# Loading the first four groups of an RMSNorm-GELU kernel as two transfers with 64 KB pieces, and gamma as one

## The chip, the cores and the metric

The kernel runs on one core of one Trainium2 chip. The metric is the device time of one execution in microseconds; lower is better. All executions quoted here are fast (granted clock 1.00). The profiled span of an execution is about 2 us shorter than the time by the clock. Each kernel has one profiled execution: that of the kernel before took 317.25 us. DVE is the vector engine, ACT the scalar engine, PE the matrix engine; SP only issues transfers here.

## The reference

```python
# x: (8, 1024, 2048) float32, gamma: (2048,) float32, eps = 1e-5
rms = np.sqrt(np.mean(x ** 2, axis=-1, keepdims=True) + eps)
out = gamma * x / rms
return 0.5 * out * (1 + np.tanh(np.sqrt(2 / np.pi) * (out + 0.044715 * out ** 3)))
```

8192 rows of 8 KB are read once and written once: 67.1 MB in, 67.1 MB out, and little arithmetic on each element.

## The kernel before

The rows are cut into 16 groups of 512. A group is one SBUF tile of 128 partitions with four rows (32 KB) each. Six such tiles ("slots") are reused in turn: load g+6 may start when store g has landed. Loads are issued from SP, stores from ACT.

```python
ROWS, SLOTS, GW, CHUNK, NARROW = 4, 6, 64, 1024, 128
...
x3 = x.rearrange("b s d -> (b s) d").rearrange("(g p r) d -> g p r d", p=P, r=R)
slot = [sbuf.tile([P, R, D], FP32, name=f"slot{i}") for i in range(SLOTS)]
flat_pieces = {0: [(0, NARROW), (NARROW, R * D)]}   # store 0 only: a 512 B piece per partition, then the rest

def load(g):
    nc.sync.dma_start(out=slot[g % SLOTS], in_=x3[g])
...
def gelu_store(g):
    # four GELU activations on ACT, one per row, then:
    for a, b in flat_pieces.get(g, [(0, R * D)]):
        nc.scalar.dma_start(out=dst[:, a:b], in_=flat[:, a:b])
...
for k in range(0, D, CHUNK):                        # gamma in two transfers of 4 KB
    nc.scalar.dma_start(out=gamma_row[...], in_=gamma[k : k + CHUNK]...)
for g in range(SLOTS):
    load(g)
# PE spreads gamma to 128 partitions in PSUM (L142)
for g in range(G + 1):
    if g < G:
        # squares of group g: two or three rows on ACT (L72), one or two on DVE (L82)
        # inverse root (L90 to L102; the power on GpSimd, L95), scale by gamma on DVE (L109)
    if g:
        gelu_store(g - 1)                           # L120, L127
        if g - 1 + SLOTS < G:
            load(g - 1 + SLOTS)                     # L68
```

The store of group 0: its first 128 elements per partition go out as a "narrow" transfer of 64 KB in all, the rest as the "wide" one.

Of the kernel before, what the change touches and what calls it, by code (L numbers as in the profile page):

```python
# [1 line left out]

# [4 lines left out]

FP32 = mybir.dt.float32
ALU = mybir.AluOpType
ACT = mybir.ActivationFunctionType  # L10

P = 128
ROWS = 4
SLOTS = 6

GW = 64
CHUNK = 1024

NARROW = 128


@with_exitstack
def kernel(
    ctx: ExitStack,
    tc: tile.TileContext,
    x: bass.AP,
    gamma: bass.AP,
    eps: bass.AP,
    out: bass.AP,
):  # L30




    nc = tc.nc
    D = x.shape[-1]
    R = ROWS
    eps_f = float(eps)
    x3 = x.rearrange("b s d -> (b s) d").rearrange("(g p r) d -> g p r d", p=P, r=R)
    o3 = out.rearrange("b s d -> (b s) d").rearrange("(g p r) d -> g p r d", p=P, r=R)  # L40
    G = x3.shape[0]

    sbuf = ctx.enter_context(tc.tile_pool(name="sbuf", bufs=1))
    psum = ctx.enter_context(
        tc.tile_pool(name="psum", bufs=1, space=bass.MemoryType.PSUM)
    )
    slot = [sbuf.tile([P, R, D], FP32, name=f"slot{i}") for i in range(SLOTS)]
    spare = sbuf.tile([P, D // GW, GW + 8], FP32, name="spare")
    gamma_row = spare[0:1]
    ones = sbuf.tile([1, P], FP32, name="ones")  # L50
    warm = sbuf.tile([1, 1], FP32, name="warm")
    power = sbuf.tile([P, R], FP32, name="power")
    ssq = sbuf.tile([P, G, R], FP32, name="ssq")
    rstd = sbuf.tile([P, G, R], FP32, name="rstd")
    ms = sbuf.tile([P, R], FP32, name="ms")
    y = sbuf.tile([P, R], FP32, name="y")
    z = sbuf.tile([P, R], FP32, name="z")
    gamma_ps = psum.tile([P, D], FP32, name="gamma_ps")
    junk = psum.tile([P, D], FP32, name="junk")

    flat_pieces = {0: [(0, NARROW), (NARROW, R * D)]}

    def on_vector(g):

        return 1 if g % 3 else 2

    def load(g):
        nc.sync.dma_start(out=slot[g % SLOTS], in_=x3[g])  # L68

    def squares(g, r, n):  # L70
        for q in range(r, r + n):
            nc.scalar.activation(  # L72
                out=junk,
                in_=slot[g % SLOTS][:, q, :],
                func=ACT.Square,
                accum_out=ssq[:, g, q : q + 1],
            )

    def squares_on_vector(g, r, n):
        for q in range(r, r + n):  # L80
            row = slot[g % SLOTS][:, q, :].rearrange("p (a b) -> p a b", b=GW)
            nc.vector.scalar_tensor_tensor(  # L82
                out=spare[:, :, 0:GW], in0=row, scalar=1.0, in1=row,
                op0=ALU.bypass, op1=ALU.mult, accum_out=ssq[:, g, q : q + 1],
            )

    def inverse_rms(g):

        v = nc.vector
        v.tensor_scalar(  # L90
            out=ms, in0=ssq[:, g, :], scalar1=1.0 / D,
            scalar2=eps_f, op0=ALU.mult, op1=ALU.add,
        )
        m_, y_, z_ = ms, y, z
        nc.gpsimd.tensor_tensor(  # L95
            out=y_, in0=m_, in1=power, op=ALU.pow
        )
        v.tensor_tensor(out=z_, in0=m_, in1=y_, op=ALU.mult)  # L98
        v.scalar_tensor_tensor(  # L99
            out=z_, in0=z_, scalar=-0.5, in1=y_, op0=ALU.mult, op1=ALU.mult  # L100
        )
        v.scalar_tensor_tensor(  # L102
            out=rstd[:, g, :], in0=z_, scalar=1.5, in1=y_,
            op0=ALU.add, op1=ALU.mult,
        )

    def scale(g, r, n):
        rows = slot[g % SLOTS][:, r : r + n, :]
        nc.vector.tensor_tensor(  # L109
            out=rows,  # L110
            in0=rows,
            in1=gamma_ps.unsqueeze(1).to_broadcast([P, n, D]),
            op=ALU.mult,
        )

    def gelu_store(g):
        flat = slot[g % SLOTS].rearrange("p r d -> p (r d)")
        dst = o3[g].rearrange("p r d -> p (r d)")
        for r in range(R):
            nc.scalar.activation(  # L120
                out=slot[g % SLOTS][:, r, :],
                in_=slot[g % SLOTS][:, r, :],
                func=ACT.Gelu_apprx_tanh,
                scale=rstd[:, g, r : r + 1],
            )
        for a, b in flat_pieces.get(g, [(0, R * D)]):
            nc.scalar.dma_start(out=dst[:, a:b], in_=flat[:, a:b])  # L127

    with tc.manual_schedule():
        for k in range(0, D, CHUNK):  # L130
            nc.scalar.dma_start(
                out=gamma_row[:, k // GW : (k + CHUNK) // GW, 0:GW],
                in_=gamma[k : k + CHUNK].rearrange("(o a b) -> o a b", o=1, b=GW),
            )
        for g in range(SLOTS):
            load(g)
        nc.gpsimd.memset(power, -0.5)  # L137
        nc.vector.memset(warm, 0.0)  # L138
        nc.vector.memset(ones, 1.0)  # L139
        nc.scalar.activation(out=warm, in_=warm, func=ACT.Gelu_apprx_tanh)  # L140
        for k in range(0, D, 512):
            nc.tensor.matmul(  # L142
                out=gamma_ps[:, k : k + 512],
                lhsT=ones,
                rhs=gamma_row[:, k // GW : (k + 512) // GW, 0:GW],
                start=True,
                stop=True,
            )
        for g in range(G + 1):
            if g < G:  # L150
                squares(g, 0, R - on_vector(g))
                squares_on_vector(g, R - on_vector(g), on_vector(g))
                if g < G - 1:
                    inverse_rms(g)
                    scale(g, 0, R)
                else:
                    scale(g, 0, 1)
                    inverse_rms(g)
                    for r in range(1, R):
                        scale(g, r, 1)  # L160
            if g:
                gelu_store(g - 1)
                if g - 1 + SLOTS < G:
                    load(g - 1 + SLOTS)


# [1 line left out]
_INS = ['x', 'gamma', 'eps']  # L168
_OUTS = [((8, 1024, 2048), 'float32')]

_NUMBERS = {'eps': 9.999999747378752e-06}


# [26 lines left out]
```

## Time and profile before

| | before |
|---|---|
| time, median of the first 3 runs | 317.63 us (317.48 to 317.71) |
| profiled span | 315.3 us |
| DVE, ACT busy | 63%, 66% |
| both DMA queues together | 99.0% of the 16 engines' time |
| first store (narrow, wide) issued | 32.61, 38.28 us |

The page and the stretches of time that carry this are shown in the prediction. One more view belongs to the start: what SP, which issues the loads, waited for (total us, times, longest), in the kernel before:

```profile
SPq L68 <- DMA out_dram<-slot: 223.1, 11, 32.5
...
SPq L68 <- DMA spare<-in_gamma_dram: 5.2, 1, 5.2
SPq L68 <- DMA slot<-in_x_dram: 4.7, 1, 4.7
```

The first line is the slots' normal recycling: a load waits until the store that frees its slot has landed. The other two are the fifth and sixth load of the start (groups 4 and 5; the prediction's "loads 5 and 6"), held up although their slots are free. The program has no dependence there, so I take it that they reuse the completion semaphores of gamma and of the first load; the view doesn't show that. They delay issues that would have stood in a queue anyway. Everywhere else "load 6" is the load of group 6.

The trace also keeps one record for each DMA packet: start, duration, queue and size. They are used below for what the page doesn't print. Their times are given in us after the first packet, which starts about 1.8 us into the span. I call a packet "stretched" by what it took beyond its size at 27.2 bytes per ns plus 8.2 ns, and sum this per engine.

### The profile page before, as it was taken

Reading aid. Unit: us, or ns where it says so; the run is one execution under the profiler, and the core shown is the slowest. Engines: PE = TensorE matmul, PEld = TensorE weight load, DVE = VectorE, ACT = ScalarE, POOL = GpSimd, SP = SyncE. Lnnn points to the kernel's source line nnn. Section 1 sums busy time; section 2 is a strip of 40 time slices with the busy share of each in tenths; the row PEclk is TensorE's granted clock in tenths of the full one; section 3 lists DMA queues with packets and bytes.
Section 4 is the critical chain, followed back from the end, with each engine's and each line's share of the span. In section 5 each row is a group of like instructions: output and inputs, shape, how many; then the busy total and the mean of one; then the engine's idle time right before and its main releaser. Section 6 shows DMA issues by size and latency. Waiting matters only on the chain.

```text
span 315.3 us, 463 instructions
## 1 busy us (share of the span) xinstructions
PE 7.2 (2%) x8; PEld 2.5 (1%) x8; DVE 198.6 (63%) x129; ACT 207.0 (66%) x150; POOL 16.4 (5%) x21
## 2 busy tenths in 40 slices
PE   0900000000000000000000000000000000000000
PEld 0300000000000000000000000000000000000000
DVE  0089889898988843927687286376934639684000
ACT  1327999999986819569292793948649397499000
POOL 0010110101010101001010010101001010010000
DMA  8999999999999999999999999999999999999996
GB/s 333 412 453 416 452 395 404 461 403 461 417 449 420 442 424 441 420 445 424 441 424 441 428 436 432 432 432 432 432 436 436 428 445 420 453 412 453 412 453 279
DMA packets 4818, 134.24 MB, mean 426 GB/s; under 512 B 592, under 2 KB 720, under 8 KB 720
## 3 DMA queue, kind: packets, MB, share of 16 engines
q1 hardware_dynamic: 2304, 67.11, 49.7%
q10 hardware_dynamic: 2512, 67.12, 49.3%
q14 instruction: 2, 0.02, 0.0%
HBM read 67.12 MB, written 67.11 MB: 426 GB/s over the span
## 4 chain that ended last, share of the span: by engine, by line
another core or an unknown queue 36%; DMA 27%; DVE 16%; ACT 7%; PE 2%; issue 2%; POOL 1%; SPq 1%; ACTq 0%; DVEq 0%; POOLq 0%
DMA out_dram<-slot 14%; DVE slot L109 11%; DMA slot<-in_x_dram 10%; ACT slot L120 7%; DVE spare L82 4%; DMA spare<-in_gamma_dram 2%; PE gamma_ps L142 2%; POOL y L95 1%; SPq L68 1%; ACT junk L72 1%; DVE ms L90 0%; DVE z L98 0%; DVE z L99 0%; DVE rstd L102 0%
## 5 line engine op out<-in xcount | busy, mean ns | idle before, releaser
L109 DVE TENSOR_TENSOR slot<-slot,gamma_ps 128x8192 f32<-128x8192 f32 (+1 forms) x19 | 139.2, 7334 | 0.0
L72 ACT ACTIVATE junk<-slot 128x2048 f32<-128x2048 f32 x42 | 79.0, 1882 | 79.8 <-DMA slot<-in_x_dram 77.4
L120 ACT ACTIVATE slot<-slot,rstd 128x2048 f32<-128x2048 f32 x64 | 122.7, 1987 | 2.8 <-DVE slot L109 2.3
L82 DVE SCALAR_TENSOR_TENSOR spare<-slot 128x2048 f32<-128x2048 f32 x22 | 50.4, 2290 | 43.6 <-DMA slot<-in_x_dram 29.1
L95 POOL TENSOR_TENSOR y<-ms,power 128x4 f32<-128x4 f32 x16 | 16.1, 1007 | 263.1 <-DVE ms L90 263.1
L90 DVE TENSOR_SCALAR ms<-ssq 128x4 f32<-128x4 f32 x16 | 2.7, 170 | 24.2 <-ACT junk L72 22.8
L98 DVE TENSOR_TENSOR z<-ms,y 128x4 f32<-128x4 f32 x16 | 2.6, 164 | 19.0 <-POOL y L95 19.0
L72 ACT ACTIVATION_READ_ACCUMULATOR junk<-slot 128x1 f32 x42 | 7.8, 186 | 0.0
L142 PE MATMUL gamma_ps<-spare,ones 1*128 1x512 f32 x8 | 7.2, 1073 | 8.1 <-DMA spare<-in_gamma_dram 8.1
L102 DVE SCALAR_TENSOR_TENSOR rstd<-z,y 128x4 f32<-128x4 f32 x16 | 2.6, 163 | 0.5
L99 DVE SCALAR_TENSOR_TENSOR z<-z,y 128x4 f32<-128x4 f32 x16 | 2.6, 163 | 0.5
L140 ACT ACT_TABLE_LOAD x1 | 1.3, 1283 | 2.0 <-issue 2.0
L142 PEld LDWEIGHTS gamma_ps<-spare,ones 1*128 1x128 f32 x8 | 2.5, 325 | 11.2 <-issue 10.7
L82 DVE DVE_READ_ACCUMULATOR spare<-slot 128x1 f32 x22 | 1.8, 82 | 0.0
L138 DVE MEMSET warm<- 1x1 f32 x1 | 0.1, 59 | 0.8 <-PEq L181 0.8
L140 ACT ACTIVATE warm<-warm 1x1 f32<-1x1 f32 x1 | 0.2, 202 | 0.0
L139 DVE MEMSET ones<- 1x128 f32 x1 | 0.2, 165 | 0.0
L137 POOL MEMSET power<- 128x4 f32 x1 | 0.1, 101 | 0.3 <-POOLq L181 0.3
L181 POOL MEMSET const-float32-0.0<- 128x1 f32 x1 | 0.1, 98 | 0.2 <-issue 0.2
L181 POOL MEMSET const-bfloat16-1.0<- 128x1 bf16 x1 | 0.1, 102 | 0.0
L181 POOL MEMSET const-uint8-127<- 128x1 uint8 x1 | 0.1, 102 | 0.0
L181 POOL MEMSET const-float32-1.0<- 128x1 f32 x1 | 0.1, 98 | 0.0
## 6 DMA issues: line engine op xcount, KB each, us to landing
slot<-in_x_dram SPq DMA_DIRECT2D x16, 4096.0 KB, 31.4
out_dram<-slot ACTq DMA_DIRECT2D x15, 4096.0 KB, 50.0
out_dram<-slot ACTq DMA_DIRECT2D x1, 4032.0 KB, 27.3
out_dram<-slot ACTq DMA_DIRECT2D x1, 64.0 KB, 13.2
spare<-in_gamma_dram ACTq DMA_DIRECT2D x2, 4.0 KB, 8.2
```

What stands on the lines that cost most here:

```text
L68: nc.sync.dma_start(out=slot[g % SLOTS], in_=x3[g])
L72: nc.scalar.activation(out=junk, in_=slot[g % SLOTS][:, q, :], func=ACT.Square, accum_out=ssq[:, g, q : q + 1],)
L82: nc.vector.scalar_tensor_tensor(out=spare[:, :, 0:GW], in0=row, scalar=1.0, in1=row, op0=ALU.bypass, op1=ALU.mult, accum_out=ssq[:, g, q ...
L90: v.tensor_scalar(out=ms, in0=ssq[:, g, :], scalar1=1.0 / D, scalar2=eps_f, op0=ALU.mult, op1=ALU.add,)
L95: nc.gpsimd.tensor_tensor(out=y_, in0=m_, in1=power, op=ALU.pow)
L98: v.tensor_tensor(out=z_, in0=m_, in1=y_, op=ALU.mult)
L99: v.scalar_tensor_tensor(out=z_, in0=z_, scalar=-0.5, in1=y_, op0=ALU.mult, op1=ALU.mult)
L102: v.scalar_tensor_tensor(out=rstd[:, g, :], in0=z_, scalar=1.5, in1=y_, op0=ALU.add, op1=ALU.mult,)
L109: nc.vector.tensor_tensor(out=rows, in0=rows, in1=gamma_ps.unsqueeze(1).to_broadcast([P, n, D]), op=ALU.mult,)
L120: nc.scalar.activation(out=slot[g % SLOTS][:, r, :], in_=slot[g % SLOTS][:, r, :], func=ACT.Gelu_apprx_tanh, scale=rstd[:, g, r : r + 1],)
L140: nc.scalar.activation(out=warm, in_=warm, func=ACT.Gelu_apprx_tanh)
L142: nc.tensor.matmul(out=gamma_ps[:, k : k + 512], lhsT=ones, rhs=gamma_row[:, k // GW : (k + 512) // GW, 0:GW], start=True, stop=True,)
```

## The change

Its intent is fewer and larger DMA pieces: groups 0 to 3 now lie as eight consecutive rows (64 KB) per partition and come in two transfers of 8 MB, gamma comes in one, so there are 32 transfers instead of 35. The stores keep 32 KB pieces, at the new places.

```diff
+PAIRS = 2
-GW = 64
-CHUNK = 1024
+GW = 128
...
+    def pair_part(a, k):
+        n = 2 * R * P
+        return a[k * n : (k + 1) * n].rearrange("(p r) d -> p r d", p=P)
+
+    def part(a, g):
+        if g < 2 * PAIRS:
+            return pair_part(a, g // 2)[:, g % 2 * R : g % 2 * R + R, :]
+        return a[g * R * P : (g + 1) * R * P].rearrange("(p r) d -> p r d", p=P)
...
-    slot = [sbuf.tile([P, R, D], FP32, name=f"slot{i}") for i in range(SLOTS)]
+    pair = [sbuf.tile([P, 2 * R, D], FP32, name=f"pair{i}") for i in range(SLOTS // 2)]
+    slot = [pair[i // 2][:, i % 2 * R : i % 2 * R + R, :] for i in range(SLOTS)]
...
-        for k in range(0, D, CHUNK):
-            nc.scalar.dma_start(  # half of gamma
...
-        for g in range(SLOTS):
-            load(g)
+        for k in range(PAIRS):
+            nc.sync.dma_start(out=pair[k], in_=pair_part(x2, k))
+        for g in range(2 * PAIRS, SLOTS):
+            load(g)
+        nc.scalar.dma_start(  # gamma in one
...
```

More of the change, by code (lines that the diff above doesn't have):

```diff
@@ L38 @@
     eps_f = float(eps)
-    x3 = x.rearrange("b s d -> (b s) d").rearrange("(g p r) d -> g p r d", p=P, r=R)
-    o3 = out.rearrange("b s d -> (b s) d").rearrange("(g p r) d -> g p r d", p=P, r=R)
-    G = x3.shape[0]
+    x2 = x.rearrange("b s d -> (b s) d")
+    o2 = out.rearrange("b s d -> (b s) d")
+    G = x2.shape[0] // (P * R)
+    def pair_part(a, k):
[5 more added lines that the diff above has]
+        return a[g * R * P : (g + 1) * R * P].rearrange("(p r) d -> p r d", p=P)
     sbuf = ctx.enter_context(tc.tile_pool(name="sbuf", bufs=1))
@@ L46 @@
     )
-    slot = [sbuf.tile([P, R, D], FP32, name=f"slot{i}") for i in range(SLOTS)]
-    spare = sbuf.tile([P, D // GW, GW + 8], FP32, name="spare")
+    pair = [
+        sbuf.tile([P, 2 * R, D], FP32, name=f"pair{i}") for i in range(SLOTS // 2)
+    ]
+    slot = [pair[i // 2][:, i % 2 * R : i % 2 * R + R, :] for i in range(SLOTS)]
+    spare = sbuf.tile([P, D // GW, GW + 16], FP32, name="spare")
     gamma_row = spare[0:1]
@@ L59 @@
     junk = psum.tile([P, D], FP32, name="junk")
-    flat_pieces = {0: [(0, NARROW), (NARROW, R * D)]}
     def on_vector(g):
@@ L67, in load @@
     def load(g):
-        nc.sync.dma_start(out=slot[g % SLOTS], in_=x3[g])
+        nc.sync.dma_start(out=slot[g % SLOTS], in_=part(x2, g))
     def squares(g, r, n):
@@ L114, in scale, with gelu @@
         )
-    def gelu_store(g):
-        flat = slot[g % SLOTS].rearrange("p r d -> p (r d)")
-        dst = o3[g].rearrange("p r d -> p (r d)")
+    def gelu(g):
         for r in range(R):
@@ L125, in gelu_store, with store @@
             )
-        for a, b in flat_pieces.get(g, [(0, R * D)]):
-            nc.scalar.dma_start(out=dst[:, a:b], in_=flat[:, a:b])
-    with tc.manual_schedule():
-        for k in range(0, D, CHUNK):
-            nc.scalar.dma_start(
-                out=gamma_row[:, k // GW : (k + CHUNK) // GW, 0:GW],
-                in_=gamma[k : k + CHUNK].rearrange("(o a b) -> o a b", o=1, b=GW),
-            )
-        for g in range(SLOTS):
+    def store(g):
+        if g:
+            nc.scalar.dma_start(out=part(o2, g), in_=slot[g % SLOTS])
+            return
+        src = pair[0].rearrange("p r d -> p (r d)")
+        dst = pair_part(o2, 0).rearrange("p r d -> p (r d)")
+        for a, z in ((0, NARROW), (NARROW, R * D)):
+            nc.scalar.dma_start(out=dst[:, a:z], in_=src[:, a:z])
+    with tc.manual_schedule():
+        for k in range(PAIRS):
+            nc.sync.dma_start(out=pair[k], in_=pair_part(x2, k))
+        for g in range(2 * PAIRS, SLOTS):
             load(g)
+        nc.scalar.dma_start(
+            out=gamma_row[:, :, 0:GW],
+            in_=gamma.rearrange("(o a b) -> o a b", o=1, b=GW),
+        )
         nc.gpsimd.memset(power, -0.5)
@@ L161 @@
             if g:
-                gelu_store(g - 1)
+                gelu(g - 1)
+                store(g - 1)
                 if g - 1 + SLOTS < G:
```

## The prediction

> **What bounds the kernel now.** I read the page first, then the DMA windows, then the start of the timeline and the waits of the SP queue.
>
> The page of the kernel before:
>
> ```profile
> span 315.3 us, 463 instructions
> ...
> PE 7.2 (2%) x8; PEld 2.5 (1%) x8; DVE 198.6 (63%) x129; ACT 207.0 (66%) x150; POOL 16.4 (5%) x21
> ...
> DMA  8999999999999999999999999999999999999996
> ...
> DMA packets 4818, 134.24 MB, mean 426 GB/s; under 512 B 592, under 2 KB 720, under 8 KB 720
> ...
> q1 hardware_dynamic: 2304, 67.11, 49.7%
> q10 hardware_dynamic: 2512, 67.12, 49.3%
> ```
>
> No compute engine is busy more than 66% of the span, while the two DMA queues together take 99.0% of the 16 engines' time, half for loads (q1) and half for stores (q10). The windows show where the remaining 1% lies (the last two columns are DMA share and GB/s; a packet counts where it starts, hence shares over 1):
>
> ```profile
> 0.00:12.00 12.00, 3.92 (x5) 1.82 (x6) 0.22 (x2) 1.49 (x2) 0.30 (x5) 1.00 0.86 350
> 12.00:24.00 12.00, 3.24 (x4) 0.66 (x2) 7.32 (x9) 5.27 (x5) 1.01 (x1) 1.00 1.01 437
> ...
> 44.00:48.00 4.00, 0.00 (x0) 0.00 (x0) 2.64 (x7) 4.00 (x4) 1.01 (x1) 1.00 0.89 318
> ...
> 160.00:200.00 40.00, 0.00 (x0) 0.00 (x0) 23.61 (x16) 26.44 (x19) 2.01 (x2) 1.00 1.00 433
> ...
> 300.00:313.00 13.00, 0.00 (x0) 0.00 (x0) 0.00 (x0) 0.00 (x0) 0.00 (x0) 1.00 0.99 426
> ```
>
> From about 1.8 us, where the first packet starts, to about 314 us, where the last ends, the engines are never empty. Only three places lose anything: the first packets, which the packet records give as 1.5 to 2.0 us instead of 1.213 us (about 0.6 us); a dip near 44 to 48 us, when the first wide store begins and two rounds of load packets stretch to 1.3 to 2.0 us (about 0.8 us per engine); and the end. The arithmetic closes: 4096 pieces of 32 KB over 16 engines are 256 each, times 1.213 us = 310.5 us, plus about 1.4 us stretched, plus small packets, is the observed 312.2 us of packet time, and 1.8 us before it and 1.3 us after it make 315.3. The time by the clock, 317.63 us, is 2.3 us longer than the profiled span; I carry that over. So the bound is bytes through the 16 engines, and only fixed costs per packet, stretched packets or an empty queue can change the time.
>
> **What the Trainium skill says.** "Perfetto Trace Analysis", section What "DMA-bound" means, separates a bound on the DMA engines from one on the issuing sequencer, and says that large descriptors are what matter for both. The trace says engines: one issue occupies SP for 0.33 us, and there are only 16 load issues. "DMA: Bandwidth & Descriptors", section Why small descriptors are slow, gives a fixed cost of about 3 cycles per packet. The trace agrees in kind: a 512 B packet took 27 ns and a 32 KB one 1.213 us, so 32256 bytes cost 1.186 us, 27.2 bytes per ns, and 32768 bytes at that rate 1.205 us; 8 ns per packet is left over. At 32 KB that is only 0.7%. The same page, Where 436 GB/s comes from, puts the ceiling at 435.2 GB/s; the steady 433 here is within 0.6% of it, so there is no rate left to win. The same page, Queues, rings and completion order, says that each engine takes the queues it has work for in turn, packet by packet; the equal shares above fit, though no line of this profile isolates the turn.
>
> **The change, part by part.** *Larger pieces.* Groups 0 to 3 are 16.8 MB: 4 x 128 = 512 pieces of 32 KB, 32 per engine, become 256 pieces of 64 KB, 16 per engine. Sixteen fixed costs of 8 ns fall away: 0.13 us. One such piece should take 65536/27.2 + 8 ns = 2.418 us (estimate) against 2 x 1.213 = 2.426.
>
> *Fewer transfers.* Two loads and one gamma transfer less: three completion packets of 9 ns per engine, and one 256 B packet of 18 ns replaced by the longer 27 ns one, so 2 x 18 - 27 = 9 ns. Together 0.04 us. All of it lies on the bound resource, so it counts: about -0.2 us.
>
> *SP's waits.* Loads 5 and 6 no longer wait for an earlier transfer's semaphore (SP waited 5.2 us on gamma and 4.7 us on a load, then was done issuing at about 13.3 us). Worth nothing: the first four loads are 39 us of queued work by then.
>
> *A later start of compute.* This is the large move. Before:
>
> ```profile
> 12.96 1.88 ACT L72 ACTIVATE junk<-slot 128x2048 f32<-128x2048 f32 x1 [9.46 <-DMA slot<-in_x_dram]
> ...
> 15.28 2.29 DVE L82 SCALAR_TENSOR_TENSOR spare<-slot 128x2048 f32<-128x2048 f32 x1 [14.26 <-PE gamma_ps L142]
> ...
> 21.86 8.68 DVE L109 TENSOR_TENSOR slot<-slot,gamma_ps 128x8192 f32<-128x8192 f32 x1
> 22.74 1.88 ACT L72 ACTIVATE junk<-slot 128x2048 f32<-128x2048 f32 x1 [5.74 <-DMA slot<-in_x_dram]
> ...
> 38.28 0.34 ACTq L127 DMA_DIRECT2D out_dram<-slot  x1
> ```
>
> Group 0 started at 12.96 us, when its 4 MB had landed, and group 1 at 22.74. Now both arrive in one transfer of 8 MB, so group 0 starts at about 22.7 us. From there: two DVE squares 4.6 us (27.3), the inverse root 2.0 (29.3), the scale 8.7 (38.0), four GELUs 7.7 (45.7). The wide first store, issued at 38.28 before, is issued at about 45.7, 7.4 us later. Later groups take 13.8 us each, ACT being the slower (three squares at 2.04 and four GELUs, 7.7), so store 1 moves from 52.3 to about 59.6.
>
> Does the DMA run dry? All six initial loads are 25.2 MB, 58 us of work alone. In the kernel before the wide store's first packet started at 47.0 us, 8.7 us after its issue (it stood behind the narrow 64 KB piece). With the same lag it starts at 54.4 now, when 22.2 MB of the loads are in and 3.0 MB remain. Shared half and half, the loads end near 68 us, and store 0 near 71. The load queue is then empty for about 6 us until load 6 (which waits for store 0) gets going, but store 1 (issued 59.6) has 4.2 MB queued and store 2 arrives at about 72. So one queue empties, the engines don't. From then on a group costs the DMA 19.4 us (8.4 MB at 433 GB/s) and ACT 13.8 us, and the lost 7.4 us are won back in about two groups.
>
> At the end, load 15 was in at about 270.5 us by its packets, with 43.5 us of stores (18.8 MB) still to be moved; the last store was issued at 291.7, 21 us later. That leaves some 13 us of slack beyond that last store's own 9.7 us, and a shift of loads against stores by 3 to 7 us does not use it up.
>
> *Gamma.* One 8 KB transfer, behind a few packets of twice the length: before, the first piece let PE start at 8.08; I allow up to 12. PE needs 7.2 us, so gamma is ready by 19, still before 22.7. Its wait is hidden.
>
> Sum: 317.63 - 0.2 = 317.4 us.
>
> **The rivals.** *The late start shows at the end.* Then 7.4 us are added: 325. For it speaks that the first store really moves; against it the 1.00 DMA share throughout, and 6 slots holding 25 MB of work. *The DMA runs dry once, near 70 us.* If the compute chain slips by another 10 us, or the tracker makes load 6 wait for both halves of its pair (store 1 too), there could be a hole of a few us: 319 to 322. The instruction list speaks against it: load 6 waits for store 0's two semaphores, not store 1's. *64 KB pieces move at another rate.* They are 39 us of work; 3% either way is 1.2 us, and 2% of the whole would need 16%. Nothing in this trace has a piece of that size, so this is the chief uncertainty. *The stretched packets.* The 0.8 us lost at the first wide store may vanish or double when it moves; it will now meet the loads of groups 4 and 5, which are still 32 KB, so I keep it.
>
> **Range and chances.** Known gain 0.2 us; stretched packets +-0.5, piece rate +-0.7, uneven ends of the 16 engines (the last one was 0.3 us behind the next) +-0.3. That gives 316.6 to 318.3. A change over 2% needs 6.4 us, which the total of all losses on the DMA (about 4.5 us with both ends) cannot give as a gain, and which as a loss only the first rival reaches.
>
> **What would show it right or wrong.** Right: packet records with 256 pieces of 64 KB at about 2.418 us, page packets down by about 320 (256 pieces, 48 completion packets, 16 gamma) to 4498; ACT's first squares near 22.7 us; the wide store issued near 45.7; DMA digits of 9 from slice 2 to 39. Wrong: a slice below 9 between 60 and 90 us, 64 KB pieces over 2.5 us, 32 KB packets still there in the first 40 us (pieces cut again), or a last store issued later than about 303 us.

## The result, and the profile after

Ratios are the mean time of one kernel's fast runs over that of the other's fast runs in the same rounds, so they are not quite the ratio of the medians quoted.

| | before | changed kernel |
|---|---|---|
| 6 runs each | 317.56 us (317.46 to 317.81) | 318.06 us (317.40 to 318.72) |
| ratio, 95% interval | | 1.0013 (0.9997 to 1.0029) |
| profiled span | 315.3 us | 315.3 us |

The same within 2%, and no difference clear of noise. What stands out is the spread: the six runs of the kernel before lie within 0.35 us, the changed kernel's within 1.3 us.

The page of the changed kernel, the lines that answer to those of before:

```profile
span 315.3 us, 454 instructions
...
DMA  9999989999999999999999999999999999999997
...
DMA packets 4498, 134.24 MB, mean 426 GB/s; under 512 B 512, under 2 KB 656, under 8 KB 656
...
q1 hardware_dynamic: 2016, 67.11, 49.8%
q10 hardware_dynamic: 2480, 67.12, 49.4%
```

320 packets are gone and the queues still fill 99.2% of the engines' time. The single 8 (slice 6, 39.4 to 47.3 us) is a matter of counting: a packet of 64 KB counts where it starts, and the last ones start at about 39.3 us, just before that slice. By the packet records the engines were idle for 0.04 us each between 35 and 60 us after the first packet.

The start of the changed kernel's timeline (start, duration, engine, line, operation; in brackets the idle time before it):

```profile
10.77 7.16 PE L162 MATMUL gamma_ps<-spare,ones 1*128 1x512 f32 x8 [10.77 <-DMA spare<-in_gamma_dram]
...
22.71 1.88 ACT L86 ACTIVATE junk<-pair 128x2048 f32<-128x2048 f32 x1 [19.85 <-DMA pair<-in_x_dram]
22.82 2.29 DVE L96 SCALAR_TENSOR_TENSOR spare<-pair 128x2048 f32<-128x2048 f32 x1 [21.81 <-DMA pair<-in_x_dram]
...
29.41 8.68 DVE L123 TENSOR_TENSOR pair<-pair,gamma_ps 128x8192 f32<-128x8192 f32 x1
...
45.83 0.34 ACTq L146 DMA_DIRECT2D out_dram<-pair  x1
```

Compute starts 9.75 us later, and the wide store is issued 7.55 us later (45.83 against 38.28). The windows of the changed kernel (last two columns DMA share and GB/s), for stretches that the prediction shows of the kernel before, for the new start of the wide store (52 to 56 us) and for the ones in which a hole was possible:

```profile
0.00:12.00 12.00, 1.23 (x2) 0.74 (x3) 0.22 (x2) 1.49 (x2) 0.31 (x5) 1.00 0.87 350
...
44.00:48.00 4.00, 0.00 (x0) 0.00 (x0) 4.00 (x1) 3.58 (x2) 0.00 (x0) 1.00 0.95 408
52.00:56.00 4.00, 0.00 (x0) 0.00 (x0) 2.64 (x7) 4.00 (x5) 1.01 (x1) 1.00 1.10 393
60.00:70.00 10.00, 0.00 (x0) 0.00 (x0) 8.64 (x8) 9.69 (x8) 1.01 (x1) 1.00 1.01 435
70.00:80.00 10.00, 0.00 (x0) 0.00 (x0) 9.97 (x4) 8.96 (x8) 0.00 (x0) 1.00 1.05 448
80.00:90.00 10.00, 0.00 (x0) 0.00 (x0) 8.64 (x7) 9.55 (x7) 1.01 (x1) 1.00 0.97 416
160.00:200.00 40.00, 0.00 (x0) 0.00 (x0) 23.11 (x14) 26.40 (x21) 1.93 (x3) 1.00 1.01 434
300.00:313.00 13.00, 0.00 (x0) 0.00 (x0) 0.00 (x0) 0.00 (x0) 0.00 (x0) 1.00 1.00 434
```

No engine time is lost to a hole. The dip of the kernel before (318 GB/s from 44 to 48 us) has moved with the wide store: 393 GB/s at a share of 1.10 from 52 to 56 us. A reader should not compare two windows of 10 us finely: packets count where they start, so one more or less round of packets at an edge moves 5%. The packet records are exact, and they show where the saving went (us per engine; "first store" is 35 to 60 us and "second lot" 70 to 90 us after the first packet):

```
                          before   changed
all packets, unstretched  310.90   310.73     -0.17, the saving
stretched: first packets    0.59     0.73
           first store      0.72     0.79
           second lot       0.02     0.18
           elsewhere        0.12     0.13
sum                       312.35   312.57     +0.22
load queue empty          -        67.3 to 74.1
```

(The printed sums differ from their parts by rounding.) The 64 KB pieces took 2.418 us in the median, exactly the estimate. The saving is there, and in this execution more than it (0.39 us) came back as stretched packets. Little of that can be pinned on the change: over the 14 traces the stretch of the first packets varies from 0.50 to 0.73 us and that of the first store from 0.66 to 1.07 (the one delayed past the loads left out). Only the second lot, between 70 and 90 us, is outside what the kernel before shows; it begins when the load queue has stood empty for 7 us. And this execution was the fastest of the six, so its packets don't show what made three others slower by 0.9 to 1.3 us.

SP's waits in the changed kernel:

```profile
SPq L82 <- DMA out_dram<-pair: 216.2, 11, 32.1
...
SPq L82 <- DMA pair<-in_x_dram: 20.0, 1, 20.0
```

The waits of 5.2 and 4.7 us are gone. The 20.0 us are not a new cost: it is load 6, whose first condition (the pair's load has landed) merely comes before the one that decides, the landing of store 0.

### The profile page after: what moved, and what is told of

Read it like the earlier page. It is cut to its first block, busy times and chain, and to the rows that moved or that the text cites. A ratio compares the mean times of both kernels' runs of the same rounds, so it can differ in the third digit from the quotient of the medians.

```text
span 315.3 us, 454 instructions
## 1 busy us (share of the span) xinstructions
PE 7.2 (2%) x8; PEld 2.5 (1%) x8; DVE 198.4 (63%) x129; ACT 207.1 (66%) x150; POOL 16.4 (5%) x21
## 4 chain that ended last, share of the span: by engine, by line
DMA 30%; another core or an unknown queue 30%; DVE 16%; ACT 12%; issue 2%; POOL 1%; SPq 1%; ACTq 0%; DVEq 0%; POOLq 0%
DMA pair<-in_x_dram 16%; DMA out_dram<-pair 14%; DVE pair L123 11%; ACT pair L132 9%; DVE spare L96 4%; ACT junk L86 3%; POOL y L109 1%; SPq L82 1%; DVE ms L104 0%; DVE z L112 0%; DVE z L113 0%; ACTq L141 0%; DVE rstd L116 0%; DVEq L104 0%
## 5 line engine op out<-in xcount | busy, mean ns | idle before, releaser
L123 DVE TENSOR_TENSOR pair<-pair,gamma_ps 128x8192 f32<-128x8192 f32 (+1 forms) x19 | 139.2, 7334 | 0.0
L86 ACT ACTIVATE junk<-pair 128x2048 f32<-128x2048 f32 x42 | 79.0, 1882 | 76.0 <-DMA pair<-in_x_dram 73.0
L132 ACT ACTIVATE pair<-pair,rstd 128x2048 f32<-128x2048 f32 x64 | 122.7, 1988 | 6.2 <-DVE pair L123 5.8
L96 DVE SCALAR_TENSOR_TENSOR spare<-pair 128x2048 f32<-128x2048 f32 x22 | 50.4, 2290 | 46.8 <-DMA pair<-in_x_dram 46.6
L86 ACT ACTIVATION_READ_ACCUMULATOR junk<-pair 128x1 f32 x42 | 7.9, 187 | 0.0
L96 DVE DVE_READ_ACCUMULATOR spare<-pair 128x1 f32 x22 | 1.8, 82 | 0.0
## 6 DMA issues: line engine op xcount, KB each, us to landing
out_dram<-pair ACTq DMA_DIRECT2D x1, 64.0 KB, 14.7
pair<-in_x_dram SPq DMA_DIRECT2D x2, 31.4
```

Source lines behind the costliest of these rows:

```text
L86: nc.scalar.activation(out=junk, in_=slot[g % SLOTS][:, q, :], func=ACT.Square, accum_out=ssq[:, g, q : q + 1],)
L96: nc.vector.scalar_tensor_tensor(out=spare[:, :, 0:GW], in0=row, scalar=1.0, in1=row, op0=ALU.bypass, op1=ALU.mult, accum_out=ssq[:, g, q ...
L123: nc.vector.tensor_tensor(out=rows, in0=rows, in1=gamma_ps.unsqueeze(1).to_broadcast([P, n, D]), op=ALU.mult,)
L132: nc.scalar.activation(out=slot[g % SLOTS][:, r, :], in_=slot[g % SLOTS][:, r, :], func=ACT.Gelu_apprx_tanh, scale=rstd[:, g, r : r + 1],)
```

## The experiments

Twelve runs, in three calls; each call's kernels ran on one chip with the kernel before beside them (medians there: 317.66, 317.49 and 317.43 us). All gave the reference's result.

**My theory** after the result: both kernels are bound by the same bytes on engines that never stand idle; the saving of 0.17 us is real; the late start of compute is absorbed, but it lets the load queue run empty, and that costs stretched packets, more in some runs than in others. **Rivals:** the 64 KB pieces themselves are uneven; the new places in memory (64 KB apart) are; the gamma part does it; or the spread was the chip's.

### The changed kernel again

No edit, five rounds.

> The changed kernel again, five rounds on one chip beside the kernel before. The theory (both are bound by the same bytes on 16 DMA engines that never run empty; the saving of 0.2 us per engine is given back in stretched packets) expects a ratio of 0.999 to 1.003, and stretched packets of 1.6 to 2.2 us per engine in the records against 1.45 of before. If the wide spread of the first six runs (317.40 to 318.72) belongs to the kernel, it comes back here: some runs over 318.2, none of before over 318.

317.32 us median, five runs from 317.24 to 317.80 and one at 318.76; ratio 0.9998 (0.9984 to 1.0012). Stretched packets 1.90 us per engine. The spread comes back in one run of six rather than three. Eleven runs of the kernel before on this chip reached at most 317.98; in all 37 of its runs two reach 318.02.

### Gamma alone

```diff
 # in the kernel before; GW = 128
-for k in range(0, D, CHUNK): nc.scalar.dma_start(...)   # two halves, ahead of the loads
 for g in range(SLOTS): load(g)
+nc.scalar.dma_start(out=gamma_row[:, :, 0:GW], in_=gamma...)   # one, after them
```

> The kernel before with gamma as one transfer, issued after the six loads. The theory expects packets 4818 - 16 - 16 = 4786 and no visible change of time: 317.5, within 0.1%, compute starting as before near 13 us. A rival, that the gamma part carries the change's effect or its spread, expects runs over 318.2 here.

317.64 us (317.28 to 317.67), ratio 0.9995 (0.9983 to 1.0007); 4786 packets, stretched 1.47 us as before. The gamma part moves nothing that these runs can show and brings no spread.

### The new places, but four transfers

```diff
 # in the changed kernel
-for k in range(PAIRS):
-    nc.sync.dma_start(out=pair[k], in_=pair_part(x2, k))
-for g in range(2 * PAIRS, SLOTS):
+for g in range(SLOTS):
     load(g)
```

> The changed kernel with groups 0 to 3 loaded by four transfers of four rows again (32 KB pieces, but still at the changed kernel's places, 64 KB apart per partition). The theory expects 317.6, the first store back near 38 us, 4498 + 256 + 32 = 4786 packets. If the spread comes from the pieces of 64 KB or the late start, it is gone here (all runs under 318); if it comes from the places in memory or the gamma part, it stays.

317.37 us (317.24 to 317.46), ratio 0.9990 (0.9978 to 1.0002). The wide store is issued at 38.41 us again, the second lot is 0.02 us, and no run is over 317.5. So neither the places in memory nor the gamma part makes the spread.

### The late start without the large pieces

```diff
 # in the changed kernel; groups at the places of the kernel before
-nc.sync.dma_start(out=pair[k], in_=pair_part(x2, k))
+nc.sync.dma_start(
+    out=pair[k].rearrange("p (g r) d -> p g (r d)", g=2),
+    in_=x2[2*k*R*P : 2*(k+1)*R*P].rearrange("(g p r) d -> p g (r d)", g=2, p=P),
+)   # still one transfer of 8 MB, in 32 KB pieces
```

> The changed kernel with the same two transfers of 8 MB, but each of two runs of 32 KB per partition, from the places of the kernel before: the late start without the 64 KB pieces. The theory expects 4498 + 256 = 4754 packets, first store near 45.8 us, and a time 0.13 us above the changed kernel's fast runs: 317.5 to 317.7. If the spread comes from the late start (a load queue that runs empty near 70 us), it stays here with runs over 318.2; if from 64 KB pieces, it goes.

318.23 us (318.02 to 318.39), ratio 1.0016 (1.0003 to 1.0029): slower than the kernel before by more than the noise, and 0.6 us above what I expected. The wide store is issued at 45.79 us, the load queue is empty from 67.2 to 74.3 us, and the second lot is 0.88 us per engine. Even the window shows it, for this kernel and then for the kernel before:

```profile
80.00:90.00 10.00, 0.00 (x0) 0.00 (x0) 8.64 (x7) 9.55 (x7) 1.01 (x1) 1.00 0.97 390
```

```profile
80.00:90.00 10.00, 0.00 (x0) 0.00 (x0) 8.64 (x8) 9.94 (x9) 1.01 (x1) 1.00 0.97 420
```

The same DMA share of 0.97 moves 390 GB/s instead of 420: the engines are busy, but their packets are stretched. This clears the 64 KB pieces and points to the transfer of 8 MB and its late landing. The edit also changes the order in which memory is read, and by itself it can't tell the two apart; the next experiments go on from there. The packet records place the lot more exactly: 0.68 of the 0.88 us fall on loads between 82 and 86.5 us, 8 to 12 us after the load queue resumed, where store 1 has ended and the engines carry only loads for 1.3 us. Such a pause between two stores stands in the kernel before as well (at 81.8 us), without a second lot.

### The large pieces without the late start of group 0

```diff
 # in the changed kernel
-for k in range(PAIRS):
-    nc.sync.dma_start(out=pair[k], in_=pair_part(x2, k))
+load(0)
+load(1)
+nc.sync.dma_start(out=pair[1], in_=pair_part(x2, 1))
```

> The changed kernel with groups 0 and 1 loaded by two transfers again and only groups 2 and 3 in one transfer of 64 KB pieces: an early start with half of the large pieces. If the late start is what takes the gain back (load queue empty for 8 us, then 0.2 to 0.9 us of stretched packets between 70 and 90 us), then those stretched packets are gone, the load queue has no gap, all runs lie under 317.8 and the median near 317.3. If the 64 KB pieces themselves do it, runs over 318.2 remain.

317.29 us (317.06 to 317.32), ratio 0.9992 (0.9980 to 1.0004); no long gap in the load queue, second lot 0.02 us.

> The kernel with only groups 2 and 3 in 64 KB pieces again. Theory: median 317.2 to 317.4, no run over 317.8, and 0.1 to 0.3 us below the kernel before in the same rounds.

317.26 us, ratio 0.9996 (0.9983 to 1.0008), with one run at 317.81 that misses the stated bound by 0.01 us. The second lot is 0.02 us again. The gain over the kernel before is not clear of noise.

A third kernel has `PAIRS = 3` beside `load(0)`, `load(1)` and a loop over pairs 1 and 2, thus as many large pieces as the changed kernel:

> Groups 0 and 1 by two transfers, groups 2 to 5 by two transfers of 64 KB pieces: as many large pieces as the changed kernel has, without its late start of group 0. Fixed costs 0.13 us per engine below the kernel before. Theory: 317.1 to 317.4 if the load queue keeps running; if group 4, which now arrives together with group 5, comes too late and empties a queue, stretched packets and runs over 318 return.

317.37 us (317.28 to 317.62), ratio 0.9998 (0.9986 to 1.0011). Its unstretched packets sum to 310.73 us, as in the changed kernel, so the saving is there; stretches at the first store took 1.07 us. And it corrects my theory: its load queue stands empty too, from 62.7 to 74.3 us, yet the second lot is 0.02 us. An empty load queue alone is not enough. In this kernel compute had started early, but its wide store's first packet was even later than the changed kernel's (55.1 us against 52.2), so the time at which that store begins doesn't decide it either. It was late because an engine's eight narrow packets took 14.9 us from first to last, beside loads of 64 KB, against 7.8 us in the kernel before.

### How late may the start be?

```diff
 # in the changed kernel, ahead of group 0's own DVE squares; n = 2 (four squares) or 5 (ten)
+if g == 0:
+    for _ in range(n):
+        squares_on_vector(g, R - 2, 2)
```

> The changed kernel with four more DVE squares of group 0 (2.33 us each, 9.3 us, same result) ahead of the first scale, so that the first wide store is issued near 55 us instead of 45.8. The theory, that a late start costs nothing as long as the first store's packets come before the six initial loads end (near 60.5 us), expects at most a small loss: 317.5 to 319, no slice below 9. A rival, that a late start of compute shows at the end in full, expects 326 to 327.

317.85 us (317.75 to 318.21), ratio 1.0015 (1.0000 to 1.0029). With another 9.3 us of delay in compute the kernel is 0.4 us above the kernel before of the same rounds, barely clear of noise, and not 9. The load queue is empty for 14 us, no engine is, and the second lot is 0.90 us, 0.89 of it between 82 and 86.5 us.

> The same with ten more squares (23.3 us): the narrow store is issued near 63.5 and the wide one near 69 us, after the loads have ended near 60.5. Now the engines must stand idle: about 5 us before the narrow piece, 5.5 before the wide one, some 3 more before load 6. The theory expects 327 to 332 us and DMA digits under 9 between 60 and 90 us. If a late start were never of consequence, it would stay at 318; if it counted in full, 341.

328.98 us (328.46 to 329.17), ratio 1.0359 (1.0346 to 1.0372), inside the stated 327 to 332. The windows of this run:

```profile
60.00:70.00 10.00, 0.00 (x0) 0.00 (x0) 8.64 (x8) 8.02 (x5) 1.01 (x1) 1.00 0.02 7
70.00:80.00 10.00, 0.00 (x0) 0.00 (x0) 8.64 (x8) 9.94 (x9) 1.01 (x1) 1.00 0.96 413
80.00:90.00 10.00, 0.00 (x0) 0.00 (x0) 9.96 (x4) 9.55 (x8) 0.00 (x0) 1.00 0.87 315
```

Now the engines do stand idle: the initial loads end 59.4 us after the first packet, the wide store begins at 68.4, and between them lies only the narrow piece. So the six loads are a reserve that lasts to about 59 us; the changed kernel begins its wide store 7 us before that, this one 9 us after. The run shows one thing more. Its first wide store starts while no load is under way, and the stretch from 68 to 79.4 us is 0.07 us instead of the 0.66 to 1.07 us at the first store elsewhere. Stretched packets (1.50 us) come instead after 79.5 us: 0.93 us on loads that set in again alone, as no wide store packet runs from 78.1 to 85.8 us, and 0.55 us when store 1 joins them. So the first store as such doesn't stretch packets, and a meeting of the two queues isn't needed either.

### The narrow piece of the first store

```diff
 # in the kernel before
-flat_pieces = {0: [(0, NARROW), (NARROW, R * D)]}
+flat_pieces = {}
```

> The kernel before with its first store in one piece, without the narrow one. In the records of every kernel so far the load packets are stretched by 0.7 to 0.9 us per engine where the narrow piece ends and the wide store begins. If the narrow piece causes that, it goes: excess near 0.75 instead of 1.45 us per engine and 316.8 to 317.0 us. If it is the first store as such that does it, the stretch stays or grows, and the time is 317.6 or more.

318.20 us (317.62 to 318.92), ratio 1.0023 (1.0009 to 1.0037). The stretch at the first store stays, 0.66 us: the narrow piece doesn't cause it. Without it the kernel before is slower and as uneven as the changed one, in two clusters (317.62 to 317.77 and 318.64 to 318.92), although its second lot is only 0.07 us. The profiled execution was of the better cluster, so what the narrow piece prevents is not seen; this stays open.

```diff
 # in the changed kernel
-for a, z in ((0, NARROW), (NARROW, R * D)):
+for a, z in ((0, R * D),):
```

> The changed kernel with its first store in one piece. The wide store should begin about 2 us after its issue at 45.8 instead of 8 us after, so store 0 lands earlier, load 6 is issued before the six initial loads have ended (near 73 us), and the load queue has no gap although compute starts as late as in the changed kernel. If the gap in the load queue is what brings the second lot of stretched packets (70 to 90 us), they fall under 0.15 us per engine; if the late start brings them in another way, 0.2 to 0.9 us stay. The time may still be 318 for the reason, not known yet, for which the kernel before lost 0.5 us without its narrow piece.

316.93 us, five runs from 316.83 to 317.09, ratio 0.9983 (0.9971 to 0.9996): here leaving the narrow piece out makes the kernel faster and steady, and this is the only version whose interval lies below the kernel before, by 0.17% (0.5 us). The wide store was issued at 45.75 us, as late as ever, but its first packet starts at 48.6 us after the first packet instead of 52.2, since it no longer queues behind the narrow one. Store 0 lands sooner, the load queue has no gap over 2.1 us (2.0 in the kernel before), and the second lot is 0.00 us. With the saving kept, the sum of packet time is 312.28 us per engine, against 312.57 in the changed kernel. Against the kernel before (312.35) that is only 0.07 us, so most of the 0.5 us is not explained by the packets. The comparison with the changed kernel itself goes through the kernel before, as they ran on different chips.

### The fixed cost of a packet

```diff
 # in the kernel before: every load in two transfers of two rows, 16 KB pieces
+for h in range(0, R, 2):
+    nc.sync.dma_start(out=slot[g % SLOTS][:, h : h + 2, :], in_=x3[g][:, h : h + 2, :])
```

> The kernel before with every load cut into two transfers of two rows: 16 KB pieces, 128 more packets per engine. If a packet costs 8 ns whatever its size, that is 1.05 us, and 0.14 us for the 16 more completion packets: 318.8 us, and 16 KB packets of 0.611 us in the records. If the packet's fixed cost is hidden, the time stays at 317.6.

A 16 KB packet took 0.611 us in the median and the unstretched sum rose from 310.90 to 312.08 us, by 1.18: the price per packet is right. But the time is 331.60 us (331.18 to 332.11), a clear miss. The DMA issues of this run (KB each, median us to landing):

```profile
slot<-in_x_dram SPq DMA_DIRECT2D x32, 2048.0 KB, 47.1
out_dram<-slot ACTq DMA_DIRECT2D x15, 4096.0 KB, 19.5
```

In the kernel before loads take 31.4 us to land and stores 50.0; here loads of half the size take 47.1 and stores 19.5. The engines take the two queues in turn packet by packet, as the Trainium skill has it ("DMA: Bandwidth & Descriptors", Queues, rings and completion order), so that a load packet of 16 KB gets half the bytes per turn of a store packet of 32 KB: from 60 to 80 us after the first packet the records show 143 GB/s of loads beside 288 of stores. Stores overtake and wait for compute (none is under way from 82.8 to 93.5 us, while loads are), compute waits for loads, and the stretch from 300 to 313 us has a DMA share of 0.65. SP's own waits for earlier loads (45.7 us in this run) are not the reason: the load queue stays filled, with no gap over 1.2 us until the loads end. The records divide the 14.7 us that the profiled span grew: 1.2 us are fixed costs, 4.6 us more stretched packets, and the rest engines that stood idle. Larger pieces gave their queue the larger share here; the changed kernel has its 64 KB pieces only while no store is under way.

## Why the prediction was right or wrong

The time was foretold at 317.4 us with a range of 316.6 to 318.3 and landed at 318.06, later at 317.32. That the second is so near is no evidence for the 0.2 us, which is 0.05% where the ratio's interval is 0.14% either way. Of the signs named, one came out otherwise: the DMA digits have an 8 in slice 6, which is the counting told above. By its steps:

- **The bound.** Right. The queues fill 99.2% of the engines' time in the changed kernel, and the two runs that moved the time by more than 2% (ten extra squares, 16 KB loads) are the two in which the engines stood idle, by the records 12.3 and 10.4 us each, against 0.7 to 1.4 us in the others.
- **The saving of 0.2 us.** Right as a cost: 310.90 to 310.73 us of unstretched packets, 0.17 where 0.17 (0.13 and 0.04) was added up, and 2.418 us per large piece. In the time it can't be seen: it is smaller than the noise of any ratio here, and the fourth point works against it.
- **The late start.** Right in every time given: squares at 22.71 (22.7), wide store issued at 45.83 (45.7), gamma's matmuls at 10.77 and hidden, load queue empty from about 69 to 76 us of the span (68 to 74). That such lateness is won back was shown by delaying compute by 9.3 us more, which left the time 0.4 us above the kernel before.
- **"So one queue empties, the engines don't", and the stretched packets kept at their old size.** This is the term that was mis-sized. The engines stay busy, yet their packets stretch: 1.84 us per engine instead of 1.45, of it 0.16 more in the second lot, 0.14 at the first packets and 0.07 at the first store; the last two are within what the traces scatter. In the kernel with the late start and 32 KB pieces the second lot is 0.88. The range allowed for this (0.5 us either way); the central value did not.
- **The spread**, which the prediction had not named. Runs over 318 came in 4 of the changed kernel's 12, in all 5 with its transfers of 8 MB in 32 KB pieces, and in none of the 25 runs of the kernels that start early with the narrow piece kept (gamma alone, four transfers, and the three runs with large pieces for later groups only). So the spread goes with the late start, but not with it alone: the changed kernel without the narrow piece starts as late and has none in 5 runs, and the kernel before without it starts early and has 3 in 6. That the slow runs of the changed kernel are those with a large second lot is only argued, as only their times are known, not their traces.
- **The rivals.** A late start that counts in full is refuted. The hole near 70 us exists only with 23 us more delay. Another rate of 64 KB pieces is refuted by their 2.418 us.

Open: what exactly stretches the second lot, which in three of the five traces that have it falls mostly 8 us and more after the load queue resumed. It came in every kernel that started late *and* let its load queue run empty (0.14 to 1.50 us); late start without the gap had none (0.00), and a gap with an early start had none (0.02). And why the narrow piece helps the kernel before and harms the changed one; for the second the delayed store 0 and the gap are shown, for the first nothing is.

## What to carry to other kernels

When the DMA engines are full from end to end, merging transfers can only win the fixed cost per packet, here 8 ns of 1213; work that out before anything else, and then ask what the larger transfer delays. A transfer that lands later may be all but absorbed and still change how the load and store queues overlap: the second lot of up to 0.9 us in two of the late kernels in which no engine ran out of work is more than the 0.17 us that the merging won. A constant tuned to the old timing (the narrow first piece) has to be tried again after such a change: leaving it out turned no gain into a small clear one.

## What the Trainium skill lacked or had wrong

- "DMA: Bandwidth & Descriptors", Why small descriptors are slow, gives about 3 cycles of overhead per packet. The records, in which a packet is one piece, give 8.2 ns, the same for 16, 32 and 64 KB, which is about 7 cycles (an estimate: the page counts 32 bytes per cycle, and 27.2 bytes per ns were measured, so a cycle is 1.18 ns).
- "Perfetto Trace Analysis", What "DMA-bound" means, says that large descriptors are what matter for a kernel bound on the engines. Going from 32 to 64 KB saved 0.3% of a piece's time and nothing clear of the whole; 16 KB cost 14 us, of which the cost per descriptor was 1.2 us and stretched packets 4.6; the rest was engines left idle as the queues fell out of order.
- "DMA: Bandwidth & Descriptors", Queues, rings and completion order, says that engines take turns between queues by packet, but not what follows for pieces of unequal size: 143 GB/s of loads in 16 KB pieces beside 288 GB/s of stores in 32 KB pieces.
- No page has the stretching of load packets around the start of a queue: 0.66 to 1.07 us per engine at the first wide store in every trace but one, 0.07 us in that one, where no load was under way, and 0.93 us there when loads set in again alone.
